# Hybrid diffusion backbone on one core: three in-projection tiles from inputs that are scaled but not yet shifted

## The chip, the cores and the metric

The kernel runs on one core of a Trainium2 chip. The core has a matrix engine (TensorE, PE in the profile), VectorE (DVE), ScalarE (ACT), GpSimd (POOL), and SyncE (SP), which here only issues transfers. Each engine takes its own instructions in the order in which the program lists them; between engines there are semaphores. The metric is the time of one execution on the device, in microseconds (us). Shares and rows come from one profiled execution.

## The reference

Two streams, 256 latent and 256 context tokens of width 1024, go through two layers. Each layer starts with an RMS norm whose result is scaled and shifted by vectors made from a conditioning vector (adaLN); layer 0 then has one large in-projection. What the change touches is this, for both streams:

```
mod_l = jnp.split((jax.nn.silu(c) @ ada_w[li] + ada_b[li])[:, None, :], 6, axis=-1)
mod_c = jnp.split(jax.nn.silu(c_ctx) @ ada_w[li] + ada_b[li], 6, axis=-1)
hl = rmsnorm(xl, norm1_g[li]) * (1.0 + mod_l[1]) + mod_l[0]
hc = rmsnorm(xc, norm1_g[li]) * (1.0 + mod_c[1]) + mod_c[0]
...
p_lat = h_lat @ w_in
p_ctx = h_ctx @ w_in
...
p = p + (centred_shift(p) - p) * mu
r, k, v, wd, ad, gd = jnp.split(p, ...)
```

`mod[0]` is the shift, `mod[1]` the scale; each is one vector of 1024 for a stream. `centred_shift` is the mean of the two neighbouring tokens. `wd` and `ad` then go through small matrices (lora) to a decay and a gate, `k` is normalised head by head (kk), and a recurrent scan follows, then attention heads, MLP, a second layer.

## The kernel before

Both streams lie side by side, 512 columns, 128 features on the partitions, so 1024 features are eight blocks j. Every product with weights is made in fp32 parts: a weight tile `rw` (four blocks k of 128x128, one DMA, L356) is copied to its high part `rh` on ACT (`actf`, L357, shown in the profile as L90) and the rest `rl` on DVE or POOL (L358); the input is split in the same way into `hh` and `hl`. `unit` multiplies one such half tile: for each of the four k, hh by rh, hl by rh, hh by rl, 12 matmuls of 128x512 into the PSUM tile `inps`. An in-projection tile is two halves (`in_half`), 24 matmuls. `w_ahead` prepares up to three half tiles ahead in the order of the list `todo`.

The start: the constants, x and ctx are loaded, then 16 pieces `araw` of 512 KB of the adaLN weights, for the shift (job (0,0)) and the scale (job (0,1)). `ada` (L180) multiplies them with `csil`, the conditioning after its silu: 32 fp32 matmuls for a job, each two records in the profile, into `adaps`. ACT copies the result to `adarow`, PE transposes it back with `ct` (a table of constants), DVE adds the bias and writes `mods`. From the scale DVE makes `gs` (gain times one plus scale). In the meantime the norms have made x times its reciprocal root, in place. Then for j in 8 and for both streams: `hh` = x·gs + shift on ACT, the same in full as `nap` on DVE (L413), `hl` = nap - hh on DVE (L414).

Then come the tables `cr` and `ca`, and a pool that takes over the space of x: the two small matrices `lora` and `gup` (L512, L514), the table `sm` (DVE, from `pk`), and a ring of four `arow` tiles (256 KB) through which three more adaLN jobs, (0,2) to (0,4), are loaded on SP's queue (L191) and multiplied bit by bit, one piece behind each step of `units`.

`units` is the list of in-projection tiles: `wda` (column 1536: wd and ad), then k, r, v of the four pairs of heads, then the gate. The PSUM tiles come from `bank`: two buffers called mm and one called x, in turn, so that a fourth tile takes the buffer of the first. `shiftmix` reads a finished tile: one ACT copy with the factor mu1, and two DVE operations over 510 columns that add the neighbours (the tiles are `wda` and `krv`). With wda, PE makes `zp` and `ap` (through lora), ACT `lt`, DVE two scans `cs`, POOL the products `BK`, `AR` and `bsum`. For kk, ACT squares k (`smq`), PE sums per head (`kkps`, eight records), DVE makes a reciprocal root in small Newton steps (`nw_x`, `nw_y`, `nw_t`), PE spreads it (`kkb`), DVE multiplies (`kk`). A table `after` says behind which step of `units` each of these is issued, so the program's order is written by hand, and every engine keeps it.

The first two tiles, wda and k of the first pair, are made together: half 0 of both, then half 1 of both.

Of the kernel before, what the change touches and what calls it, by code (L numbers as in the profile page):

```python
# [7 lines left out]
F32 = mybir.dt.float32  # L8
# [9 lines left out]
D = 1024  # L18
# [33 lines left out]
def build(ctx: ExitStack, tc, xT, cT, pk_d, ct_d, ca_d, cs_d, lora_d, gup_d, cb_d, ada_w, adaT, w_in, w_out, w1, w2,  # L52
# [24 lines left out]
    def tt(o, a, b, op):  # L77
        dve.tensor_tensor(o, a, b, op)  # L78

    def ts(o, a, s1, op0, s2=None, op1=None):  # L80
        if op1 is None:
            dve.tensor_scalar(o, a, s1, None, op0)
        else:
            dve.tensor_scalar(o, a, s1, s2, op0, op1)

    def stt(o, a, s, b, op0, op1):
        dve.scalar_tensor_tensor(o, a, s, b, op0, op1)  # L87

    def actf(o, i, f, scale=1.0, bias=0.0, **kw):
        act.activation(out=o, in_=i, func=f, scale=scale, bias=bias, **kw)  # L90

    def psm(shape, name="mm"):
        return PS["mm"].tile(shape, F32, name=name, tag="mm")
# [175 lines left out]
    def norm_add(acc, x):  # L269

        a, _, n = acc
        acc[2] += 1
        if n == 0:
            actf(a, x, AF.Square)
        else:
            sq = gen.tile([128, T], F32, name="sq", tag="sq" if n < 7 else "nap", bufs=2)
            actf(sq, x, AF.Square)
            if n < 7:
                tt(a, a, sq, ADD)
            else:  # L280
                acc[1] = sq
# [46 lines left out]
    with ExitStack() as c1:  # L328
# [12 lines left out]
            return reg.tile(shape, F32, name=name, tag="r4", bufs=6)  # L341

        wv = kview(w_in)
        todo, ready = [], []

        def w_unit():

# [3 lines left out]
        def w_ahead(n):  # L351
            while todo and len(ready) < n:
                v, c, k, eng = todo.pop(0)
                r, h, l = (reg.tile([128, 4, 128], dt, name=nm, tag=nm, bufs=b)
                           for nm, dt, b in (("rw", F32, 3), ("rh", F32R, 3), ("rl", F32R, 3)))
# [13 lines left out]
        def in_half(ps, i):  # L369
            unit(ps, hh, hl, 4 * i, i == 0, i == 1)  # L370

        def enqueue(v, cols, ks=(0, 4), engs=(pool,)):
            todo.extend((v, c, k, engs[i % len(engs)]) for i, c in enumerate(cols) for k in ks)

        for k in (0, 4):
            enqueue(wv, [1536, 512], (k,), (dve,))
        enqueue(wv, [0, 1024], (0, 4), (dve,))
# [6 lines left out]
        def split(src, hi, lo):  # L384
            actf(hi, src, AF.Copy)
            tt(lo, src, hi.bitcast(F32), SUB)

        with tc.tile_pool(name="x0", bufs=1) as xp:
            x0 = [xp.tile([128, 8, T], F32, name=f"x0{s}") for s in range(2)]
            nc.sync.dma_start(out=x0[0], in_=xT)  # L390
            nc.sync.dma_start(out=x0[1], in_=cT)
# [5 lines left out]
            gs = {}  # L397
            for s in range(2):
                acc = norm_acc(xp, s)
                for j in range(8):  # L400
                    norm_add(acc, x0[s][:, j])
                pb = norm_rstd(acc)
                for j in range(8):
                    tt(x0[s][:, j], x0[s][:, j], pb, MUL)
                gs[s] = gen.tile([128, 8], F32, name="gs", tag="gs", bufs=2)
                stt(gs[s], mods[0][:, 1, s], 1.0, PV("n1")[:, 0:8], ADD, MUL)
            for j in range(8):
                for s in range(2):
                    c = slice(s * T, s * T + T)
                    t = gen.tile([128, T], F32, name="nap", tag="nap", bufs=2)  # L410
                    m_ = gs[s][:, j:j + 1], mods[0][:, 0, s, j:j + 1]
                    actf(hh[:, j, c], x0[s][:, j], AF.Identity, scale=m_[0], bias=m_[1])
                    ts(t, x0[s][:, j], m_[0], MUL, m_[1], ADD)  # L413
# [93 lines left out]
        with tc.tile_pool(name="prep", bufs=1) as pp:  # L507
# [25 lines left out]
            rot = [0]  # L533

            def bank():

                rot[0] += 1
                return PS["x"].tile([128, NT], F32, name="inps", tag="x") if rot[0] % 3 == 0 else psm([128, NT], "inps")

            def shiftmix(n, o, ps=None):  # L540
                if ps is None:
                    ps = bank()
                    in_half(ps, 0)
                    yield
                    in_half(ps, 1)
                p3 = lambda a: a.rearrange("p (s t) -> p s t", s=2)
                actf(o, ps, AF.Identity, scale=mu1[:, n:n + 1])
                for i, j in ((slice(0, T - 1), slice(1, T)), (slice(1, T), slice(0, T - 1))):
                    stt(p3(o)[:, :, j], p3(ps)[:, :, i], muh[:, n:n + 1], p3(o)[:, :, j], MUL, ADD)

            def kk_norm(hp, k):

# [104 lines left out]

            def units():

                p2 = [bank() for _ in range(2)]  # L660
                for i in range(2):
                    for ps in p2:
                        in_half(ps, i)
                    yield
                yield from shiftmix(12, wda, p2.pop(0))
                actf(wda[0:64], wda[0:64], AF.Tanh)
                yield
                for hp in range(4):
                    krvs.append([])
                    for sec in (1, 0, 2):  # L670
                        krvs[hp].append(ring("krv", [128, NT], 6))
                        yield from shiftmix(4 * sec + hp, krvs[hp][-1], p2.pop() if p2 else None)
# [1015 lines left out]
```

## Time and profile before

| | us |
|---|---|
| runs | 1421.06, 1425.53, 1426.71 (median 1425.53) |
| the profiled execution, its own time | 1426.16 |
| its span | 1424.4 |
| PE busy | 1348.7 |
| DVE, ACT, POOL busy | 1046.4, 632.3, 264.5 |
| mean granted clock of TensorE | 0.974 |

The span is the time from the first instruction of the core to the last; starting and ending the program makes up the rest of the profiled execution's own time. Rows of groups give an operation as "out<-in", with partitions x elements and a type; a bracket behind a row of the timeline tells how long the engine had been idle and what released it. Helpers issue most instructions, so many rows have the same line (L75 matmul, L90 ACT, L78, L84 and L87 DVE); they are told apart by the tiles' names. In the timeline SPq is SP's queue of transfers and PEld the loading of weights.

### The profile page before, as it was taken

Reading aid. Unit: us, or ns where it says so; the run is one execution under the profiler, and the core shown is the slowest. Engines: PE = TensorE matmul, PEld = TensorE weight load, DVE = VectorE, ACT = ScalarE, POOL = GpSimd, SP = SyncE. Lnnn points to the kernel's source line nnn. Section 1 sums busy time; section 2 is a strip of 40 time slices with the busy share of each in tenths; the row PEclk is TensorE's granted clock in tenths of the full one; section 3 lists DMA queues with packets and bytes.
Section 4 is the critical chain, followed back from the end, with each engine's and each line's share of the span. In section 5 each row is a group of like instructions: output and inputs, shape, how many; then the busy total and the mean of one; then the engine's idle time right before and its main releaser. Section 6 shows DMA issues by size and latency. Waiting matters only on the chain.

```text
span 1424.4 us, 25962 instructions
## 1 busy us (share of the span) xinstructions
PE 1348.7 (95%) x10026; PEld 1139.4 (80%) x10026; DVE 1046.4 (73%) x2245; ACT 632.3 (44%) x1186; POOL 264.5 (19%) x196
## 2 busy tenths in 40 slices
PE   6899998999998799999999998999999989999997
PEld 2566666777887788888888997888888879999997
DVE  3788869756778899887666577697778785766665
ACT  2534434444543543223232243765645533555543
POOL 0122342211004200000000001233323335311100
PEclk9999998899999899999999999999999999999998
DMA  9566574134323466666666433754444423566663
GB/s 350 171 187 185 185 200 111 60 77 171 104 85 112 133 201 186 192 191 200 207 195 215 145 103 88 180 146 134 133 119 133 110 84 106 153 186 187 184 185 97
DMA packets 311324, 220.42 MB, mean 155 GB/s; under 512 B 30176, under 2 KB 279840, under 8 KB 310048
## 3 DMA queue, kind: packets, MB, share of 16 engines
q1 hardware_dynamic: 306080, 210.36, 49.8%
q10 hardware_dynamic: 3968, 4.20, 1.0%
q0 software_dynamic: 1152, 4.19, 0.8%
q8 instruction: 79, 1.29, 0.4%
q14 instruction: 45, 0.37, 0.1%
HBM read 205.54 MB, written 13.17 MB: 154 GB/s over the span
## 4 chain that ended last, share of the span: by engine, by line
PE 61%; DVE 5%; ACT 1%; issue 1%; DVEq 0%; ACTq 0%
PE m L75 38%; PE xsp L75 5%; PE zp L75 3%; PE bm L75 3%; PE so L75 3%; PE first L75 1%; PE cm L75 1%; PE ssdy L75 1%; PE hst L75 1%; PE xtp L1434 1%; PE nps L75 0%; DVE cva L87 0%; PE gn L75 0%; PE hlat L75 0%; PE gnb L75 0%
## 5 line engine op out<-in xcount | busy, mean ns | idle before, releaser
L90 ACT ACTIVATE wh<-wraw 128x1024 fp32r<-128x1024 f32 x197 | 208.2, 1058 | 366.4 <-PE m L75 255.6
L75 PE MATMUL m<-hid,wh 128*128 128x256 f32 (+1 forms) x1152 | 256.5, 318 | 0.6 <-DVE hid L78 0.6
L146 POOL TENSOR_TENSOR wl<-wraw,wh 128x1024 fp32r<-128x1024 f32 x55 | 133.2, 2428 | 614.5 <-ACT wh L90 602.5
L146 DVE TENSOR_TENSOR wl<-wraw,wh 128x1024 fp32r<-128x1024 f32 x142 | 173.7, 1223 | 43.8 <-ACT wh L90 43.7
L75 PEld LDWEIGHTS m<-hid,wh 128*128 128x128 f32 x1152 | 190.5, 189 | 17.0 <-DVE hid L78 0.8
L75 PE MATMUL m<-hid,wl 128*128 128x256 f32 (+1 forms) x576 | 183.3, 318 | 0.0
L75 PEld LDWEIGHTS m<-hid,wl 128*128 128x128 f32 x576 | 108.8, 189 | 7.7
L75 PE MATMUL m<-hh,wh 128*128 128x512 f32 (+1 forms) x264 | 103.3, 394 | 0.0
L75 PE MATMUL m<-hh,wl 128*128 128x512 f32 (+1 forms) x264 | 103.1, 393 | 0.0
L75 PE MATMUL m<-hl,wh 128*128 128x512 f32 (+1 forms) x264 | 103.1, 393 | 0.0
L246 DVE CUSTOM_DVE_ANT_0 arow<-arow,cb 128x512 f32<-128x512 f32 x112 | 75.9, 689 | 27.2 <-DMA arow<-in_adaT_dram 26.1
L358 POOL TENSOR_TENSOR rl<-rw,rh 128x512 fp32r<-128x512 f32 x45 | 59.9, 1333 | 187.2 <-ACT rh L90 177.2
L75 PE MATMUL inps<-hh,rh 128*128 128x512 f32 x208 | 90.2, 435 | 2.7 <-ACT hh L90 2.7
L90 ACT ACTIVATE rh<-rw 128x512 fp32r<-128x512 f32 x73 | 45.5, 627 | 95.2 <-PE inps L75 63.1
L75 PE MATMUL inps<-hl,rh 128*128 128x512 f32 x208 | 85.7, 413 | 0.2 <-DVE hl L78 0.2
L75 PE MATMUL inps<-hh,rl 128*128 128x512 f32 x208 | 85.2, 410 | 0.0
L75 PE MATMUL m<-uh,wh 128*128 128x258 f32 x256 | 73.4, 287 | 2.4 <-ACT uh L90 2.4
L75 PE MATMUL m<-ul,wh 128*128 128x258 f32 x256 | 73.3, 286 | 0.0
L75 PE MATMUL m<-uh,wl 128*128 128x258 f32 x256 | 73.2, 286 | 0.0
L75 PEld LDWEIGHTS m<-hh,wh 128*128 128x128 f32 x264 | 50.7, 192 | 11.2
L75 PEld LDWEIGHTS m<-hh,wl 128*128 128x128 f32 x264 | 50.5, 192 | 11.5
L75 PEld LDWEIGHTS m<-hl,wh 128*128 128x128 f32 x264 | 50.5, 192 | 11.1
(690 smaller groups left out, 3340.9 us busy)
## 6 DMA issues: line engine op xcount, KB each, us to landing
wraw<-in_w_dram SPq DMA_DIRECT2D x133, 512.0 KB, 3.9
arow<-in_adaT_dram SPq DMA_DIRECT2D x112, 256.0 KB, 3.3
wraw<-in_s_in_dram SPq DMA_DIRECT2D x48, 512.0 KB, 4.3
rw<-in_w_in_dram SPq DMA_DIRECT2D x52, 256.0 KB, 3.6
arow<-in_ada_w_dram SPq DMA_DIRECT2D x48, 256.0 KB, 3.5
araw<-in_ada_w_dram SPq DMA_DIRECT2D x16, 512.0 KB, 9.3
csb<-csd SPq DMA_DIRECT2D x8, 1024.0 KB, 6.3
wraw<-in_s_out_dram SPq DMA_DIRECT2D x16, 512.0 KB, 3.8
```

The source lines that it names most:

```text
L75: pe.matmul(o, lhsT=l, rhs=r, start=start, stop=stop)
L90: act.activation(out=o, in_=i, func=f, scale=scale, bias=bias, **kw)
L146: eng.tensor_tensor(l, raw, h.bitcast(F32), SUB)
L246: dve.tensor_tensor_reduce(r if s == ns - 1 else junk, r, cb[:, s, i * W:i * W + W], 0.5, 0.0, MUL, ADD, sums[:, s, j, i:i + 1])
L358: eng.tensor_tensor(l, r, h.bitcast(F32), SUB)
L1434: pe.transpose(tp[:, q, i * 128:i * 128 + 128], xs[:, i, t0:t0 + 128], ident)
```

## The change

The scale is computed first, the shift second. As soon as the scale is there, x·gs alone is split, without the shift: blocks 0 to 3 into `hh` and `hl`, blocks 4 to 7 into a tile `pv_` (ACT for the high part, one DVE operation for the rest). With these the first three tiles (columns 1536, 512 and 0, the list `p3`) are multiplied, half 0 from hh and hl, half 1 from pv_. The matmuls of the shift's job run among them. The weights of these three tiles stay as they were loaded, in six tiles `er` in the pool of the x0 section. When the shift is there, 24 small fp32 matmuls multiply it with er (`bps`, 128x2 each), ACT copies them to `bsb`, and `shiftmix` adds bsb to the three tiles per stream, 256 columns at a time, in PSUM. For all other tiles hh and hl are built again with the shift, as before. x0 moves to a space (`ar`) of a longer-lived pool and `pv_` to another (`bk`).

```
-            run((ada([(0, 0), (0, 1)], araw, D), 1))
+            A = ada([(0, 1), (0, 0)], araw, D)
+            run((islice(A, 5), 1))
             w_ahead(3)
+            run((islice(A, 4), 1))
...
             for j in range(8):
                 for s in range(2):
                     c = slice(s * T, s * T + T)
+                    g = gs[s][:, j:j + 1]
+                    ph, pl = (pv_[:, 0, j - 4, c], pv_[:, 1, j - 4, c]) if j > 3 else (hh[:, j, c], hl[:, j, c])
+                    actf(ph, x0[:, s, j], AF.Copy, scale=g)
+                    stt(pl, x0[:, s, j], g, ph.bitcast(F32), MUL, SUB)
+            p3 = [bank() for _ in range(3)]
+            for ps in p3:
+                unit(ps, hh, hl, 0, True, False)
+                run((islice(A, 3), 1))
+            run((A, 1))
+            w_ahead(3)
+            bps = psg([128, 3, 2], "bps")
+            for t in range(3):
+                for k in range(8):
+                    mm(bps[:, t], er[:, 3 * (k // 4) + t, k % 4], mods[0][:, 0, :, k], k == 0, k == 7)
+            actf(bsb, bps, AF.Copy)
+            for ps in p3:
+                unit(ps, pv_[:, 0], pv_[:, 1], 0, False, True)
+            for j in (0, 1, 2, 3, 4, 5, 6, 7):
...
-            def shiftmix(n, o, ps=None):
-                if ps is None:
+            def shiftmix(n, o):
+                if p3:
+                    i, ps = 3 - len(p3), p3.pop(0)
+                    for s in range(2):
+                        c = slice(s * T, s * T + T)
+                        actf(ps[:, c], ps[:, c], AF.Identity, bias=bsb[:, i, s:s + 1])
+                else:
                     ps = bank()
...
             def units():
 
-                p2 = [bank() for _ in range(2)]
-                for i in range(2):
-                    for ps in p2:
-                        in_half(ps, i)
-                    yield
-                yield from shiftmix(12, wda, p2.pop(0))
+                yield
+                yield
+                yield from shiftmix(12, wda)
```

On PE, behind the transposition that ends the first adaLN job, there stood before:

```order
L75 MATMUL adaps<-ct,adarow 128x8 x2
L75 MATMUL adaps<-araw,csil 32x256 x32
L75 MATMUL adaps<-ct,adarow 128x8 x2
L75 MATMUL inps<-hh,rh 128x512 x2
L75 MATMUL inps<-hl,rh 128x512
```

and now:

```order
L75 MATMUL adaps<-ct,adarow 128x8 x2
L75 MATMUL inps<-hh,rh 128x512 x3
L75 MATMUL adaps<-araw,csil 32x256
L75 MATMUL inps<-hl,rh 128x512
L75 MATMUL inps<-hh,rl 128x512
```

The first products now come right behind the first transposition, and the 32 matmuls (64 records) of the second job are spread among them.

Further on PE, where the shift is ready, and then where the three tiles end and the fourth begins, the changed order has (the names ending in a number are tiles of that name: pv_ and mods):

```order
L75 MATMUL adaps<-ct,adarow 128x8 x2
L75 MATMUL inps<-pv__98,rh 128x512
L75 MATMUL inps<-pv__98,rl 128x512
L75 MATMUL bps<-mods_79,er 128x2 x24
L75 MATMUL inps<-pv__98,rh 128x512 x2
...
L75 MATMUL inps<-pv__98,rl 128x512
L75 MATMUL adaps<-arow,csil 32x2x64 x44
L75 MATMUL inps<-hh,rh 128x512
```

The 24 matmuls of bps stand ahead of the last 27 products of the three tiles, and 44 matmuls on arow, which were spread among products before in pieces of four and eight, stand in one row ahead of the fourth tile.

On ACT, at the same place of the program, before:

```order
L90 ACTIVATE adarow<-adaps 128x256 x2
L90 ACTIVATE rh<-rw 128x512
L90 ACTIVATE hh<-x_100,mods_79,gs 128x256
L90 ACTIVATE rh<-rw 128x512 x2
L90 ACTIVATE hh<-x_101,mods_79,gs 128x256
```

and now, from the second adarow on:

```order
L90 ACTIVATE adarow<-adaps 128x256
L90 ACTIVATE rh<-er 128x512 x2
L90 ACTIVATE hh<-x_97,mods_79,gs 128x256
L90 ACTIVATE bsb<-bps 128x6
L90 ACTIVATE hh<-x_97,mods_79,gs 128x256
L90 ACTIVATE rh<-rw 128x512
L90 ACTIVATE hh<-x_97,mods_79,gs 128x256 x4
L90 ACTIVATE rh<-rw 128x512
L90 ACTIVATE hh<-x_97,mods_79,gs 128x256 x10
L90 ACTIVATE inps<-inps,bsb 128x256 x6
L90 ACTIVATE wda<-inps,sm 128x512
```

The copy of bps stands between the first and the second hh with the shift; the other fifteen come behind it, and the six additions of bsb behind them.

On DVE, in the changed program, from kkps's result to the last Newton step:

```order
L84 TENSOR_SCALAR nw_x<-kkps 128x8
L84 TENSOR_SCALAR nw_y<-nw_x 128x8
L84 TENSOR_SCALAR lt<-lt 128x512
L78 TENSOR_TENSOR nw_t<-nw_y,nw_x 128x8
L641 SCALAR_TENSOR_TENSOR cs<-cr,lt 128x256 x2
L78 TENSOR_TENSOR nw_t<-nw_t,nw_y 128x8
...
L78 TENSOR_TENSOR nw_t<-nw_t,nw_y 128x8
L87 SCALAR_TENSOR_TENSOR bsum<-bsum,sm,krv 128x256
L87 SCALAR_TENSOR_TENSOR nw_y<-nw_t,nw_y 128x8
```

The scans cs and the operations on lt, which all stood ahead of nw_x before, now stand among the Newton steps.

More of the change, by code (lines that the diff above doesn't have):

```diff
@@ L353, in w_ahead @@
                 v, c, k, eng = todo.pop(0)
-                r, h, l = (reg.tile([128, 4, 128], dt, name=nm, tag=nm, bufs=b)
-                           for nm, dt, b in (("rw", F32, 3), ("rh", F32R, 3), ("rl", F32R, 3)))
+                r, h, l = (raws_.pop(0) if raws_ and nm == "rw" else reg.tile([128, 4, 128], dt, name=nm, tag=nm, bufs=3)
+                           for nm, dt in (("rw", F32), ("rh", F32R), ("rl", F32R)))
                 nc.sync.dma_start(out=r, in_=v[:, k:k + 4, c:c + 128])
@@ L375, in build @@
         for k in (0, 4):
[L376 to L377 removed]
+            enqueue(wv, [1536, 512, 0], (k,), (dve,))
+        enqueue(wv, [1024], (0, 4), (dve,))
         for hp in range(1, 4):
@@ L386, in split, with bank @@
             tt(lo, src, hi.bitcast(F32), SUB)
+        rot = [0]
+        def bank():
+            rot[0] += 1
+            return PS["x"].tile([128, NT], F32, name="inps", tag="x") if rot[0] % 3 == 0 else psm([128, NT], "inps")
+        x0 = mid.tile([128, 2, 8, T], F32, name="x0", tag="ar")
+        pv_ = mid.tile([128, 2, 4, NT], F32R, name="pv_", tag="bk")
+        bsb = reg.tile([128, 3, 2], F32, name="bsb")
         with tc.tile_pool(name="x0", bufs=1) as xp:
-            x0 = [xp.tile([128, 8, T], F32, name=f"x0{s}") for s in range(2)]
-            nc.sync.dma_start(out=x0[0], in_=xT)
-            nc.sync.dma_start(out=x0[1], in_=cT)
+            for s, v in enumerate((xT, cT)):
+                nc.sync.dma_start(out=x0[:, s], in_=v)
+            er = xp.tile([128, 6, 4, 128], F32, name="er")
+            raws_.extend(er[:, i] for i in range(6))
             i = iter(range(16))
             araw = lambda sh, n: r4(sh, n) if next(i) % 3 else xp.tile(sh, F32, name=n, tag="araw", bufs=3)
-            run((ada([(0, 0), (0, 1)], araw, D), 1))
+            A = ada([(0, 1), (0, 0)], araw, D)
+            run((islice(A, 5), 1))
             w_ahead(3)
+            run((islice(A, 4), 1))
             hh, hl = halloc()
-            gs = {}
+            gs = []
             for s in range(2):
@@ L400, in build @@
                 for j in range(8):
-                    norm_add(acc, x0[s][:, j])
+                    norm_add(acc, x0[:, s, j])
                 pb = norm_rstd(acc)
                 for j in range(8):
-                    tt(x0[s][:, j], x0[s][:, j], pb, MUL)
-                gs[s] = gen.tile([128, 8], F32, name="gs", tag="gs", bufs=2)
+                    tt(x0[:, s, j], x0[:, s, j], pb, MUL)
+                gs.append(gen.tile([128, 8], F32, name="gs", tag="gs", bufs=2))
                 stt(gs[s], mods[0][:, 1, s], 1.0, PV("n1")[:, 0:8], ADD, MUL)
@@ L409, in build @@
                     c = slice(s * T, s * T + T)
+                    g = gs[s][:, j:j + 1]
[18 more added lines that the diff above has]
+                    c = slice(s * T, s * T + T)
                     t = gen.tile([128, T], F32, name="nap", tag="nap", bufs=2)
                     m_ = gs[s][:, j:j + 1], mods[0][:, 0, s, j:j + 1]
-                    actf(hh[:, j, c], x0[s][:, j], AF.Identity, scale=m_[0], bias=m_[1])
-                    ts(t, x0[s][:, j], m_[0], MUL, m_[1], ADD)
+                    actf(hh[:, j, c], x0[:, s, j], AF.Identity, scale=m_[0], bias=m_[1])
+                    ts(t, x0[:, s, j], m_[0], MUL, m_[1], ADD)
                     tt(hl[:, j, c], t, hh[:, j, c].bitcast(F32), SUB)
@@ L532, in build @@
                 pool.memset(e[:, :, 65:66], 1.0)
[L533 to L538, printed above, removed]
-            def shiftmix(n, o, ps=None):
-                if ps is None:
+            def shiftmix(n, o):
+                if p3:
+                    i, ps = 3 - len(p3), p3.pop(0)
+                    for s in range(2):
+                        c = slice(s * T, s * T + T)
+                        actf(ps[:, c], ps[:, c], AF.Identity, bias=bsb[:, i, s:s + 1])
+                else:
                     ps = bank()
@@ L671, in units @@
                         krvs[hp].append(ring("krv", [128, NT], 6))
-                        yield from shiftmix(4 * sec + hp, krvs[hp][-1], p2.pop() if p2 else None)
+                        if hp == 0 and sec == 0:
+                            yield
+                        yield from shiftmix(4 * sec + hp, krvs[hp][-1])
                         yield
```

6 lines of the change are left out of this document (3 added, 3 removed).

## The prediction

> **What bounds the kernel now.** I read the page first (busy shares, the 40 slices), then the time in windows around the in-projection, then TensorE's waits there, then the timeline row by row.
>
> ```profile
> PE 1348.7 (95%) x10026; PEld 1139.4 (80%) x10026; DVE 1046.4 (73%) x2245; ACT 632.3 (44%) x1186; POOL 264.5 (19%) x196
> ...
> PE   6899998999998799999999998999999989999997
> ```
>
> TensorE (PE) is busy 95% of the span, and only the first slices leave it much room. The change works between 28 and 92 us, so I cut that stretch into stages (columns: window, its length, busy time of PE, weight loads, DVE, ACT, POOL, granted clock, DMA share, GB/s).
>
> ```profile
> 27.90:35.30 7.40, 7.40 (x64) 2.09 (x63) 0.18 (x1) 0.00 (x0) 0.00 (x0) 1.00 0.95 310
> 35.30:39.30 4.00, 0.72 (x9) 0.55 (x5) 2.59 (x8) 3.11 (x7) 0.00 (x0) 1.00 0.07 23
> 39.30:43.10 3.80, 3.63 (x9) 2.48 (x10) 3.80 (x12) 3.80 (x9) 0.00 (x0) 0.56 0.69 193
> 43.10:54.20 11.10, 11.08 (x47) 8.36 (x45) 10.30 (x34) 6.22 (x13) 0.22 (x4) 1.00 0.36 123
> 54.20:92.50 38.30, 37.49 (x326) 24.44 (x325) 27.41 (x49) 16.59 (x37) 10.04 (x10) 1.00 0.72 218
> 92.50:200.00 107.50, 105.24 (x856) 74.47 (x856) 78.11 (x147) 44.56 (x100) 36.33 (x38) 1.00 0.59 179
> ```
>
> PE works 98% of every window except the second, and in the third it gets 0.56 of its clock. What ended PE's waits between 27.8 and 92.6:
>
> ```profile
> PE inps L75 <- ACT hh L90: 2.7, 1, 2.7
> PE adaps L75 <- ACT adarow L90: 0.6, 1, 0.6
> PE adaps L75 <- DMA arow<-in_ada_w_dram: 0.6, 1, 0.6
> PE zp L75 <- ACT TT L90: 0.2, 1, 0.2
> PE inps L75 <- DVE hl L78: 0.2, 1, 0.2
> ```
>
> That is 4.3 us of waits. In the third window the clock costs 3.8 x 0.44 = 1.7 us more. **So 6.0 us is all that a better order can win here**; anything that it adds to PE is to be set against this.
>
> **The start.** Rows of the timeline (start, duration, engine, line, operation, tiles, count, idle time before and its releaser):
>
> ```profile
> 27.79 7.59 PE L75 MATMUL adaps<-araw,csil 128*32 128x256 f32 x64
> 27.97 0.18 DVE L78 TENSOR_TENSOR mods<-adaps,pk 128x16 f32<-128x16 f32 x1 [1.32 <-PE adaps L75]
> ...
> 36.67 0.17 DVE L78 TENSOR_TENSOR mods<-adaps,pk 128x16 f32<-128x16 f32 x1 [8.53 <-PE adaps L75]
> ...
> 38.63 7.48 ACT L90 ACTIVATE hh<-x,mods,gs 128x256 fp32r<-128x256 f32 x15
> 39.27 0.87 PE L75 MATMUL inps<-hh,rh 128*128 128x512 f32 x2 [2.70 <-ACT hh L90]
> ```
>
> From the second vector (36.67) to the first product (39.27) it is 2.6 us. In the changed order the scale comes first, so its vector is there at 27.97, and the first product stands at 30.6, with the same 2.7 us gap on PE: the 64 matmuls for the shift, which filled 27.79 to 35.38, now stand in PE's order *behind* the first products, and PE takes its instructions in order. The early gap is therefore moved, not closed. What goes is the second transposition's 0.6, the 0.2 for hl and, because of other waits below, the 0.6 for arow and 0.2 for zp: **-1.6 us**.
>
> The clock went with the gap:
>
> ```profile
> 40.00:41.00 1.00, 0.83 (x3) 0.60 (x3) 1.00 (x4) 1.00 (x3) 0.00 (x0) 0.50 0.49 129
> ```
>
> After the 2.70 us gap PE ran at 0.50. Elsewhere in the same trace a gap as long left the clock alone:
>
> ```profile
> 430.71 0.36 PE L75 MATMUL wo<-mh,rh 128*128 128x256 f32 x1 [2.73 <-DVE x L87]
> 430.70:433.43 2.73, 2.72 (x17) 2.44 (x18) 2.49 (x8) 1.10 (x3) 0.39 (x1) 1.00 0.59 182
> ```
>
> So a gap of this length may or may not be followed by half the clock. The gap at 28 is as that at 37: PE idles but for one transposition. I leave the 1.7 us where they were: 0. If the clock stays up, 1.7 us are won; if it falls behind a later gap too, 1.7 are lost. The Trainium skill (TensorE: Matmul & The Clock Gate, "Part 1: The HAM clock gate") has the half clock set in after at least one idle window of about 3.4 us, on windows that run free; taken literally, 2.7 us would never be enough, and this trace disagrees once (0.50 behind 2.70 us) and agrees once (1.00 behind 2.73 us). By that rule the sum below would be 1.7 us less.
>
> **What is added on DVE and ACT before the shift is there.** Sixteen more copies on ACT (15 took 7.48, 0.50 each: 8.0 us) and sixteen products x·gs - hh on DVE.
>
> ```profile
> L84 DVE TENSOR_SCALAR nap<-x,gs,mods x16: 405/408/411, 37.6 to 48.4; 128x256 f32<-128x256 f32 x16
> L78 DVE TENSOR_TENSOR hl<-nap,hh x16: 417/418/422, 39.5 to 49.1; 128x256 fp32r<-128x256 f32 x16
> ```
>
> The nearest rows are these 0.41 and 0.42 us, so 6.7 us. Both engines stand idle in 27.90:35.30 (0.18 and 0.00 busy of 7.40), and that hides them: 0. Without this cover, 6.7 us at most. The six er tiles are 1.5 MB loaded in front of or between the last araw tiles; 1 MB of it at 310 GB/s is 3.4 us that the last araw comes later, but PE reaches that one near 50 instead of 35: 0.
>
> **The 24 small matmuls (bps).** The bias needs er times shift in full fp32, two records each, 48 records with 2 columns. The trace has the same kind in kkps:
>
> ```profile
> 64.73 0.95 PE L75 MATMUL kkps<-cr,smq 128*128 128x2 f32 x8
> 65.60 1.12 PE L75 MATMUL adaps<-arow,csil 128*32 128x128 f32 x16
> 66.65 0.50 PE L75 MATMUL inps<-hh,rh 128*128 128x512 f32 x1
> 66.99 0.40 PE L75 MATMUL inps<-hl,rh 128*128 128x512 f32 x1
> 67.22 0.40 PE L75 MATMUL inps<-hh,rl 128*128 128x512 f32 x1
> ```
>
> Eight records take 0.87 until the next row starts, 0.109 each. 48 x 0.109 = **+5.2 us** on PE, with no other work beside it. The bounds are the nearest rows: 0.066 a record as in arow (1.05 for 16), 3.2; 0.119 by the row's whole 0.95, 5.7. I take kkps, whose shape it is. A product inps takes 0.23 (66.99 to 67.22), and 0.11 more behind small matmuls (66.65 to 66.99); with as much on the way in, an estimate, a visit of small matmuls costs 0.2 beside its records.
>
> Where this stands: 30.6 + 64 shift matmuls (7.4) + 45 of the 72 products of the three tiles (10.5) + the transposition (0.5) + six visits at 0.2 (1.2) + the cold clock 1.7 = 51.9. bps ends at B = **57.1**.
>
> **First new wait: the fourth tile.** ACT's copy bsb<-bps stands between the first and the second shifted hh. Fifteen hh, all hl behind them on DVE, six half-tile bias adds and the three shiftmixes queue behind the end of bps, B. The fourth tile takes the bank of the first one (two banks plus one take turns), so it waits for the last wda operation on DVE.
>
> ```profile
> 51.78 1.53 DVE L87 SCALAR_TENSOR_TENSOR wda<-inps,sm,wda 128x510 f32<-128x510 f32 x2
> ...
> 60.48 0.84 ACT L90 ACTIVATE lt<-zp,sm 128x256 f32<-128x256 f32 x2 [4.05 <-PE zp L75]
> ```
>
> On DVE: from the first nap (37.6) to the last hl (49.1 + 0.4) there are 11.9 us for 16 pairs with two weight parts rl among them, 0.74 a pair; 15.5 pairs make 11.5. Small sm operations 0.6, then wda, krv, wda at 0.76: 2.3. That is B + 14.4. ACT delivers at the same time: 0.2 + 15 x 0.50 + two rh at 0.6 + six adds at 0.42 + wda and krv 1.2 = 12.6, and the two rh wait about a microsecond for buffers that the products behind bps give back. So B + 14.4 to 15.5.
>
> In the meantime PE has 27 products (6.3) and, standing ahead of the fourth tile, 44 small matmuls on eleven arow tiles (88 records at 0.066, 5.8): 12.1 us. The gap is 2.3 to 3.4.
>
> **Second new wait, at the same place: arow.** SP's loads of lora, gup and arow lie in space that er leaves, and wait for bps too.
>
> ```profile
> 48.90 0.34 SPq L512 DMA_DIRECT2D lora<-in_lora_dram  x1
> ...
> 54.81 0.65 PE L75 MATMUL adaps<-arow,csil 128*32 128x128 f32 x8 [0.56 <-DMA arow<-in_ada_w_dram]
> ...
> DMA to landing us min/median/max: 2.6/3.6/5.6
> ```
>
> From lora's issue to the first arow matmul 5.9 us. Now lora goes out at B, not 48.90. Ring of four: tiles 1 to 4 at B + 5.9, 5 to 8 one reload later (3.6 + 0.5), 9 to 11 another, and three tiles' matmuls: 5.9 + 4.1 + 4.1 + 1.6 = B + 15.7. At 2.6 a reload it is 13.7, at 5.6 it is 19.7. Both chains thus end by B + 15.5, either one covers the other, and I take **+3.4 us** (1.6 to 7.6). Seven separate visits of arow become one, six saved where six came in above: 0.
>
> **Third new wait: kkb.** In the old trace kkps ended at 65.6 and kkb, behind Newton steps on DVE, began 7.0 us later.
>
> ```profile
> 65.09 1.28 POOL L633 TENSOR_TENSOR BK<-lt,cs 128x512 f32<-128x512 f32 x1 [15.86 <-DVE lt L78]
> 66.34 1.19 POOL L642 TENSOR_TENSOR bsum<-lt 128x256 f32<-128x256 f32 x1
> 68.52 1.52 POOL L635 TENSOR_TENSOR AR<-krv,e 128x256 f32<-128x256 f32 x2 [0.99 <-DVE nw_t L78]
> ...
> 68.47 1.01 DVE L87 SCALAR_TENSOR_TENSOR bsum<-bsum,sm,krv 128x256 f32<-128x256 f32 x1
> ...
> 72.64 1.09 PE L75 MATMUL kkb<-ct,nw_y 128*64 128x128 f32 x16
> ```
>
> Then PE had 31 products, and 32 small records, to fill these 7.0 us. Now between kkps and kkb stand 19 products and a zp: 4.8 us. On DVE the steps are strewn among lt, the two scans cs, rl and bsum, and bsum waits for POOL, where AR (1.52) and BK (1.28) now stand ahead of it (1.19): I count 8.8 instead of 7.0. The gap is 2.2 to 4.0; **+3.5 us**.
>
> **The sum.** -1.6 + 5.2 + 3.4 + 3.5 = **+10.5 us**. Behind kkb the rows of both orders soon agree, and with PE at 98% (92.50:200.00) a delay has nowhere to be made good. By the clock: kkb ends at B 57.1 + 15.5 + 3.7 (five products, zp, ap and kkps) + 8.8 + 1.1 = 86.2. In the old trace 18.8 us lay between kkb's end and
>
> ```profile
> 92.50 0.61 PE L75 MATMUL adaps<-ct,adarow 128*128 128x8 f32 x4
> ```
>
> of which some 2.2 us, nine products with what lies between them, have now gone in front of it; 86.2 + 16.6 = 102.8, a delay of 10.3. Of the two I take **+10.4 us**. The profiled execution took 1426.16 us (span 1424.4), 0.6 over the median of 1425.53. 1425.53 + 10.4 gives **1436 us**.
>
> **Rivals.**
> 1. *The filler is enough (not slower).* PE never starves behind bps, since its early products ran while DVE and ACT stood idle, and since hh and hl, which ACT and DVE rebuild, need not be complete for a tile to begin. Price: -1.6 + 5.2 = +3.6, 1429.1; with the gap at 28 us and its cold clock closed as well (2.7 + 1.7), -0.8, 1424.7. For it: PE's share is 98% everywhere else. Against: the copy bsb stands ahead of 15 hh, and both chains at B + 15.5 against 12.1 us of work. It decides where the two later gaps together stay under 3.5 us (7.1 - 3.6). Chance 0.24.
> 2. *arow lands late.* At 5.6 a reload the eleven tiles end at B + 19.7 instead of 15.5: +10.4 + 4.2 = +14.6, 1440.1, and 1441.8 with half the clock behind the gap. For it: 5.6 is in the row. Against: the median is 3.6. Chance 0.15.
> 3. *The clock stays up behind the first gap*, as at 430.71: +10.4 - 1.7 = +8.7, 1434.2. Chance 0.10.
> 4. *The change wins*, the three tiles being out of the way before the shift arrives: for over 0.5% it would have to save 7.1 us; 6.0 are there, and bps takes 5.2. Chance 0.03.
>
> That the change doesn't do what it says is excluded by the order of PE's rows: the products stand ahead of the shift.
>
> **How the numbers follow.** The forecast, +8 to +12, has 0.48. Range: rival 1's upper part at the low end (1427.5), rival 2 at the high end (1441.5). 0.5%, 7.1 us, is about what a measurement can tell from no change. Slower by more: nearly all of the forecast (0.43), rival 2 (0.15) and most of rival 3 (0.08): 0.66. Within: rival 1 and the lower edges, 0.30. Faster: 0.04.
>
> **What would show it.** Right: first inps near 30.6 with a 2.7 us wait; a bps row of 5 to 6 us ending near 57; lora issued just then; PE waiting for arow, then for kkb; the transposition of 92.50 near 102. Wrong: PE's wait list from 55 to 90 adds up to under 4 us, bps under 3 us, or lora issued before bps ends.

## The result and the profile after

| | before | changed |
|---|---|---|
| median of the runs, us | 1426.03 (4 runs, 1421.06 to 1426.71) | 1446.03 (4 runs, 1443.96 to 1449.19) |
| ratio, 95% interval | | 1.0136 [1.0111, 1.0160] |
| span of the profiled execution, us | 1424.4 | 1443.9 |
| PE busy, us | 1348.7 | 1361.4 |

The changed kernel is slower by 20 us. That is the direction of the forecast, but twice its size (+10.4), and outside its range. The page of the changed kernel, busy time and share by engine:

```profile
PE 1361.4 (94%) x10074; PEld 1147.9 (80%) x10074; DVE 1051.6 (73%) x2261; ACT 641.4 (44%) x1209; POOL 264.7 (18%) x196
```

What TensorE waited for there between 26 and 125 us (total, times, longest):

```profile
PE adaps L75 <- DMA arow<-in_ada_w_dram: 3.4, 3, 1.4
PE kkb L75 <- DVE nw_y L87: 2.7, 1, 2.7
PE inps L75 <- ACT hh L90: 2.5, 1, 2.5
PE zp L75 <- ACT wda L90: 1.2, 1, 1.2
```

The waits are about those that were forecast: 2.5 at the first product, 3.4 for arow, 2.7 for kkb. With two more, of 0.5 and 0.2, they are 10.5 us together, where the kernel before had 4.8 in the same stretch (24.4 to 101.9 us there), and so cannot be the surprise. TensorE's busy time has grown by 12.7 us although only 48 records were added. The timeline of TensorE in the changed kernel shows where:

```profile
28.86 0.61 PE L75 MATMUL adaps<-ct,adarow 128*128 128x8 f32 x4 [0.50 <-ACT adarow L90]
31.99 1.65 PE L75 MATMUL inps<-hh,rh 128*128 128x512 f32 x3 [2.52 <-ACT hh L90]
...
55.07 7.96 PE L75 MATMUL bps<-mods,er 128*128 128x2 f32 x48
62.88 1.20 PE L75 MATMUL inps<-pv__98,rh 128*128 128x512 f32 x2
...
71.62 2.05 PE L75 MATMUL adaps<-arow,csil 128*32 128x128 f32 x32
75.04 1.28 PE L75 MATMUL adaps<-arow,csil 128*32 128x128 f32 x16 [1.36 <-DMA arow<-in_ada_w_dram]
...
81.70 0.50 PE L75 MATMUL inps<-hh,rh 128*128 128x512 f32 x1
...
94.28 1.13 PE L75 MATMUL kkb<-ct,nw_y 128*64 128x128 f32 x16 [2.72 <-DVE nw_y L87]
...
115.59 0.61 PE L75 MATMUL adaps<-ct,adarow 128*128 128x8 f32 x4
```

bps takes 7.81 us (62.88 - 55.07), 0.163 a record and not 0.109. The 27 products behind it take 8.74 (71.62 - 62.88), not 6.3. The row of 92.50 stands at 115.59, +23.1 (+21.5 when both are measured from the first transposition, at 27.25 and 28.86). The granted clock in windows of the same profile (window, length, busy time of PE, weight loads, DVE, ACT, POOL, granted clock, DMA share, GB/s):

```profile
30.80:36.80 6.00, 4.81 (x10) 2.84 (x11) 5.98 (x15) 6.00 (x16) 0.00 (x0) 0.50 0.96 308
55.10:57.60 2.50, 2.50 (x25) 2.50 (x24) 2.06 (x5) 0.49 (x1) 0.00 (x0) 1.00 0.02 7
57.70:67.40 9.70, 9.70 (x37) 8.73 (x37) 2.57 (x7) 3.26 (x7) 0.22 (x4) 0.50 0.35 109
67.60:71.60 4.00, 4.00 (x17) 2.93 (x16) 2.23 (x6) 2.89 (x6) 0.00 (x0) 0.96 0.49 182
95.40:101.80 6.40, 6.40 (x24) 4.40 (x24) 5.77 (x12) 2.94 (x6) 0.00 (x0) 0.50 0.28 83
```

TensorE is 100% busy from 55 on, and yet 2.6 us into bps its clock falls to half, and stays there for 10 us. The half clock comes also at the first gap, where it now lasts 6.8 us (30.4 to 37.2) instead of 3.4, and behind the wait for kkb.

These changes come in steps. Cut into windows of 3.413 us with one edge at 57.66, the stretch from 20 to 1420 us has 410 of them, and in each the clock is 1.00 or 0.50 and never between; the same holds for the kernel before, with an edge at 39.72. So the 2.6 us are not a threshold: they are the place in bps at which a step came. In the other six profiles of kernels whose bps has two columns the fall comes 1.6 to 4.1 us behind the start of bps.

So two theories went into the experiments. **N**: matmuls with two columns stream so little that the clock treats TensorE as idle; bps lowers the clock on itself and on what follows. **W**: each bps record is slow since it loads a new fp32 weight block, and the clock falls for another reason. The experiments on the waits ask in addition what makes the fourth tile late: arow, or the hold, which is the time for which ScalarE keeps the building of hh and hl waiting. In the trace of each run I read when a row comes; times of runs are medians, against 1425.3 to 1426.8 of the kernel before on the same chip.

### The profile page after: what moved, and what is told of

Read it like the earlier page. It is cut to its first block, busy times and chain, and to the rows that moved or that the text cites. A ratio compares the mean times of both kernels' runs of the same rounds, so it can differ in the third digit from the quotient of the medians.

```text
span 1443.9 us, 26083 instructions
## 1 busy us (share of the span) xinstructions
PE 1361.4 (94%) x10074; PEld 1147.9 (80%) x10074; DVE 1051.6 (73%) x2261; ACT 641.4 (44%) x1209; POOL 264.7 (18%) x196
## 4 chain that ended last, share of the span: by engine, by line
PE 59%; DVE 5%; ACT 1%; issue 1%; DMA 0%; POOL 0%; DVEq 0%; ACTq 0%; POOLq 0%
PE m L75 37%; PE xsp L75 5%; PE zp L75 3%; PE bm L75 3%; PE so L75 1%; PE first L75 1%; PE cm L75 1%; PE ssdy L75 1%; PE hst L75 1%; PE xtp L1466 1%; DVE cva L87 0%; DVE ul L87 0%; PE nps L75 0%; DVE acc L78 0%; PE gn L75 0%
## 5 line engine op out<-in xcount | busy, mean ns | idle before, releaser
L75 PE MATMUL inps<-hh,rh 128*128 128x512 f32 x196 | 85.5, 438 | 2.5 <-ACT hh L90 2.5
L90 ACT ACTIVATE rh<-rw 128x512 fp32r<-128x512 f32 x67 | 42.0, 628 | 93.4 <-PE inps L75 56.6
L75 PE MATMUL inps<-hl,rh 128*128 128x512 f32 x196 | 81.0, 413 | 0.0
L75 PE MATMUL inps<-hh,rl 128*128 128x512 f32 x196 | 80.2, 409 | 0.0
L75 PEld LDWEIGHTS m<-hh,wh 128*128 128x128 f32 x264 | 50.9, 193 | 11.2
## 6 DMA issues: line engine op xcount, KB each, us to landing
araw<-in_ada_w_dram SPq DMA_DIRECT2D x16, 512.0 KB, 10.2
```

Of the source, the lines that this page charges most:

```text
L75: pe.matmul(o, lhsT=l, rhs=r, start=start, stop=stop)
```

## Experiments

**1. Without bps.** The matmuls and the copy are replaced by zeros.

```
-            bps = psg([128, 3, 2], "bps")
...
-            actf(bsb, bps, AF.Copy)
+            pool.memset(bsb, 0.0)
```

> Leaves out the shift's part in the three early tiles: no bps matmuls, bsb is zero. Read at the transposition row that stood at 92.50 before and at 115.59 in the changed kernel. Theory N (narrow matmuls let TensorE's clock fall): what goes is the 7.8 us of bps and the 2.4 us that the products behind it lost at half clock; these products then end near 61.5 instead of 71.6, the arow loads go out near 56 instead of 63, and the row stands near 107 (-8 to -10); granted clock 1.00 from 55 to 63. Rival W (bps is slow because each record reloads fp32 weights, and the half clock has another cause): -5 to -6, and the products behind still run at half clock.

Measured: 1437.6 us, ratio to the kernel before 1.0090 [1.0060, 1.0120]. Lora is issued at 56.05. The window over the 27 products in this run:

```profile
54.50:61.40 6.90, 6.83 (x29) 5.17 (x28) 6.82 (x19) 6.64 (x14) 0.32 (x4) 1.00 0.55 175
```

The clock holds. In its timeline the transposition of 115.59 stands at

```profile
104.81 0.61 PE L75 MATMUL adaps<-ct,adarow 128*128 128x8 f32 x4
```

10.8 us earlier, with the first transposition where it was (28.80). N gave 8 to 10, W 5 to 6. With what it holds up behind it, bps thus costs twice the 5.2 us at which I had priced it; and 12.3 us of the 23.1 are not its own. This is read from the rows: the times are 8.5 us apart, but the two intervals overlap at their edges (1.0111 and 1.0120).

**2. bps with 64 times the columns.** The same weights, each shift column repeated 64 times.

```
-            bps = psg([128, 3, 2], "bps")
+            bps = psg([128, 3, 2, 64], "bps")
...
-                    mm(bps[:, t], er[:, 3 * (k // 4) + t, k % 4], mods[0][:, 0, :, k], k == 0, k == 7)
+                    mm(bps[:, t], er[:, 3 * (k // 4) + t, k % 4],
+                       mods[0][:, 0, :, k:k + 1].to_broadcast([128, 2, 64]), k == 0, k == 7)
```

> The same 24 matmuls on the same weights, but with the two shift columns each repeated 64 times, so 128 columns instead of 2; nothing else is left out. Theory N: 64 times the columns and yet faster: the 48 records take 5 to 6.3 us instead of 7.8 and the granted clock stays at 1.00 through them and the products behind them (6.3 instead of 8.7 us). Rival W: at least the same 7.8 us, clock 0.50 behind as before.

Measured: 1437.4 us, 1.0072 [1.0048, 1.0096]: clear of the changed kernel's 1.0136 [1.0111, 1.0160]. The row of bps in this run's timeline, and its windows over bps and over the products behind it:

```profile
52.15 5.56 PE L75 MATMUL bps<-mods,er 128*128 128x128 f32 x48
```

```profile
52.20:57.50 5.30, 5.30 (x50) 5.30 (x49) 5.30 (x16) 5.30 (x11) 0.00 (x0) 1.00 0.01 3
57.70:64.20 6.50, 6.50 (x36) 4.89 (x34) 6.50 (x19) 5.61 (x13) 0.22 (x4) 1.00 0.83 266
```

More work on the same weights, and it is faster: 5.56 instead of 7.96 us, at clock 1.00 to the end. The weight loads are the same 48, so W falls and N stands. All the profiles agree: in the seven whose bps has two columns the clock falls within bps, in the three with 128 columns (experiments 2, 9 and 11) it stays at 1.00 to its end. Nor is it the rest of the other engines: in experiment 8 ScalarE and VectorE work all through bps, and with two columns the clock falls all the same. The order behind bps changed too in this kernel (20 arow matmuls in a row, not 44, and hh ahead of bsb), so only the rows of bps and of the clock are laid to the columns alone, and not the whole 8.6 us.

**3. Only 32 columns.** As before, with 16 in place of 64, which leaves the order nearly alone.

> As the run with 128 columns, but each shift column only 16 times: 32 columns instead of 2, with nearly the changed kernel's own order (40 arow matmuls in a row instead of 44). Theory N, if it is the number of columns that keeps the clock up by degrees: between the two, 48 records in 5.5 us and the clock at 1.00 if 32 columns are enough, 7 to 8 us with 0.50 from about 3 us on if they are not. If the clock stays up, kkb starts 4 to 5 us earlier than the changed kernel's 94.28, with the order left as it is. Rival W: 7.8 us either way.

The row of bps and two windows over it:

```profile
53.99 7.30 PE L75 MATMUL bps<-mods,er 128*128 128x32 f32 x48
```

```profile
54.00:56.60 2.60, 2.60 (x25) 2.60 (x25) 2.60 (x7) 1.49 (x3) 0.00 (x0) 1.00 0.03 6
57.50:61.30 3.80, 3.80 (x19) 3.80 (x20) 0.00 (x0) 0.00 (x0) 0.00 (x0) 0.50 0.00 0
```

Measured: 1442.4 us, 1.0111 [1.0085, 1.0137]. 32 columns are not enough: full clock at first, then half, as with two. A record of 128 columns costs 0.066 us in the arow rows and one of narrow columns, like kkps, 0.109 at full clock. So 128 columns fill at most some 60% (0.066 / 0.109) of TensorE's time in bps and 32 columns some 15%, both estimates. Where between them the clock turns was not tried.

**4. The copy bsb behind the hh.** One instruction moves on ScalarE; the line `actf(bsb, bps, AF.Copy)` stands behind the loop that builds hh and hl.

> Only the copy bsb<-bps moves on ScalarE from between the first and second shifted hh to behind the sixteenth. hh and hl are then built from 55 to 67 instead of from 63 to 78. If the hold of hh sets the start of the fourth tile (81.70 in the changed kernel), that start comes 4 us or more earlier. If the arow matmuls ahead of it set it (their last piece lands at 79.7), it stays within 1 us of 81.7 and the row of 115.59 within 1 us.

Measured: 1450.0 us, 1.0163 [1.0129, 1.0197], the fourth tile at 82.95, 53.9 after the first transposition (52.8 in the changed kernel), and the row at 115.47. Nothing is won. ScalarE's rows in the changed kernel, and those of a later run with the copy moved (experiment 7), tell why:

```profile
63.06 0.18 ACT L90 ACTIVATE bsb<-bps 128x6 f32<-128x6 f32 x1 [7.47 <-PE bps L75]
63.13 0.59 ACT L90 ACTIVATE hh<-x,mods,gs 128x256 fp32r<-128x256 f32 x1
64.17 0.63 ACT L90 ACTIVATE rh<-rw 128x512 fp32r<-128x512 f32 x1 [0.45 <-ACT hh L90]
...
68.71 0.63 ACT L90 ACTIVATE rh<-rw 128x512 fp32r<-128x512 f32 x1 [1.94 <-PE inps L75]
```

```profile
63.28 0.63 ACT L90 ACTIVATE rh<-rw 128x512 fp32r<-128x512 f32 x1 [7.99 <-issue]
```

Right behind the second hh stands a copy of the next weights, rh<-rw. It needs one of three rh buffers, and these come free only when products behind bps have read them: the profile names such a product as releaser of the later copy, at 68.71, and none for the one at 63.28. With bsb out of the way ScalarE stands in front of this copy just as long, 7.99 us for 7.47.

**5. er in a space of its own.**

```
+        erp = cp.enter_context(tc.tile_pool(name="erp", bufs=1))
...
-            er = xp.tile([128, 6, 4, 128], F32, name="er")
+            er = erp.tile([128, 6, 4, 128], F32, name="er")
```

> The er tiles get a space of their own, so lora and arow need not wait for bps: lora is issued near 55 instead of 63.05, TensorE no longer waits for arow (3.4 us in the changed kernel). If arow sets the fourth tile, it starts 4 us or more earlier than 81.70. If the hold of hh by bsb sets it (the last wda operation ends at 80.2), it starts near 80.3, 1.4 us earlier, and the row of 115.59 comes to 114.

Measured: 1443.0 us, 1.0118 [1.0094, 1.0141], not to be told from the changed kernel. The queue of transfers in this run and in the changed kernel:

```profile
52.49 0.33 SPq L548 DMA_DIRECT2D lora<-in_lora_dram  x1
...
53.34 23.87 SPq L191 DMA_DIRECT2D arow<-in_ada_w_dram  x11
```

```profile
63.05 0.33 SPq L547 DMA_DIRECT2D lora<-in_lora_dram  x1
...
63.91 14.48 SPq L191 DMA_DIRECT2D arow<-in_ada_w_dram  x11
```

The loads begin 10.6 us earlier, and yet their row ends at the same place, 49.5 us behind the first transposition (27.71 here) in both, and TensorE still waits 3.4 us for arow. The fifth arow needs a buffer of the ring of four, and gets it when TensorE has used the first, which it does only behind all products of the three tiles: four loads are issued at once, the fifth at 71.3 (72.3 in the changed kernel), each time 0.7 us behind TensorE's first arow matmul. It is the ring that makes arow late, not the late start.

**6. and 7. No arow ahead of the fourth tile; alone (arow_later), and with the copy bsb late (hold_and_arow).**

```
-                    if u > 1:
+                    if u > 6:
                         next(A, None)
```

> The changed kernel, with the arow matmuls begun five steps later, so that none stands ahead of the fourth tile (their 5.8 us come later). If the hold of hh by bsb is a second cause as late as arow, the fourth tile starts near 80.3 (wda's last operation), 1.4 us earlier than 81.70, TensorE idles 8 us there, and the time is 2 to 5 us longer. If arow alone made it late, the fourth tile starts near 72 and the time is 3 us shorter.

> Both at once: the copy bsb behind the sixteenth hh, and no arow ahead of the fourth tile. If each covered the other, the fourth tile starts at 72 to 75 and kkb 6 to 9 us earlier than 94.28, and the time is 2 to 4 us shorter than the changed kernel's 1446 (5.8 us of arow work come later). If neither matters, the fourth tile stays near 80.

Measured: 1454.3 us, 1.0206 [1.0181, 1.0230], and 1456.7 us, 1.0208 [1.0179, 1.0236]. TensorE's timeline, first without arow alone and then with both edits:

```profile
80.27 0.77 PE L75 MATMUL inps<-hh,rh 128*128 128x512 f32 x1 [8.68 <-DVE wda L87]
```

```profile
79.59 0.77 PE L75 MATMUL inps<-hh,rh 128*128 128x512 f32 x1 [8.68 <-DVE wda L87]
```

The hold is a second cause as late as arow (80.27, as expected of it), and bsb alone is not what makes it: with bsb late the same 8.68 us. The times are longer than I had thought, 8 and 11 us more than the changed kernel's, instead of 2 to 5 more and of a gain. Part of it is the clock again: with nothing to do in this wait TensorE has 0.50 from 74.0 to 87.7 in both runs, where the changed kernel has 1.00. It works 7.4 us of that in arow_later, half of which, 3.7 us, is an estimate of the loss.

**8. All hh ahead of the weight copies (hh_first_arow).** As 7, but the loop that builds hh and hl stands in front of the products behind bps, so that ScalarE's copies rh<-rw come behind it.

> As hold_and_arow (no arow ahead of the fourth tile, copy bsb late), but all sixteen shifted hh also stand ahead of ScalarE's next weight copies rh<-rw, which wait for one of three rh buffers that the products behind bps give back. If these copies are the hold, hh and hl are done by 67, under bps, and the fourth tile starts at 73 to 75 instead of 79.6, and the time is 4 to 6 us shorter than the 1454 to 1457 of the two runs without arow. If the hold lies elsewhere, the fourth tile stays near 79.6.

The timeline of ScalarE and of TensorE in this run:

```profile
54.84 7.97 ACT L90 ACTIVATE hh<-x,mods,gs 128x256 fp32r<-128x256 f32 x16
```

```profile
75.81 0.77 PE L75 MATMUL inps<-hh,rh 128*128 128x512 f32 x1 [4.21 <-DVE wda L87]
```

Measured: 1451.6 us, 1.0181 [1.0157, 1.0205]. All sixteen hh run under bps, and the fourth tile starts 46.3 us after the first transposition, not 50.9. So the copies were a hold behind bsb, and half of the 8.68 us: with bsb alone out of the way nothing goes, with both 4.5 us. The copies alone, with bsb left in its place, were not tried. The 4.21 us that stay are in ScalarE's queue too: its wda copy, at 72.88, stands behind a bias addition that waits for the third tile's products until 71.63. The time is 5 us below that of 7, with intervals that overlap.

**9. 128 columns, bsb late, arow three steps later (combo4).**

> 128 columns for bps, the copy bsb last, arow begun three steps later. By theory N with both waits gone: bps 5.6 us at full clock, fourth tile by 66 to 68, time 1432 to 1436, still above the 1426.8 of the kernel before, since bps stays and the first gap of 2.5 us too. If the waits are made up elsewhere: 1437, as with 128 columns alone.

Measured: 1443.7 us, 1.0128 [1.0106, 1.0150], so slower than with the columns alone. The fourth tile waits 4.31 us for wda until 70.72, with no arow matmuls to fill the wait, and the clock is at 0.50 for 10.2 us from 69.8 on: as in 6, moving arow away costs more than it gives.

**10. Four matmuls into the first gap (warm).** The changed kernel with matmuls that nobody reads.

```
+            fo = psg([128, 2, 256], "fill")
+            for _ in range(4):
+                mm(fo, ident, mods[0][:, 1, :, 0:1].to_broadcast([128, 2, 256]))
             p3 = [bank() for _ in range(3)]
```

> The changed kernel with four more matmuls of 128x512 in the 2.5 us gap ahead of the first product, into a bank that nobody reads (about 0.5 us each, from arow's 0.066 a record of 128 columns). Theory N (the clock follows how much TensorE has streamed): the granted clock stays at 1.00 from 30 to 37 instead of 0.50, and bps starts 2 to 3.4 us earlier after the first transposition than the 26.2 us of the changed kernel. Rival (a gap's length alone decides, or the stall of the products does): the clock falls all the same and nothing is won.

TensorE's timeline in this run, and a window over the products behind the gap:

```profile
30.24 3.70 PE L75 MATMUL fill<-mods,ct 128*128 128x512 f32 x8 [0.34 <-DVE mods L78]
...
52.09 6.57 PE L75 MATMUL bps<-mods,er 128*128 128x2 f32 x48
```

```profile
33.40:37.00 3.60, 3.60 (x18) 2.36 (x20) 3.60 (x10) 3.60 (x10) 0.00 (x0) 1.00 1.15 287
```

The clock stays up, as N has it and its rival has not, and bps begins 22.8 us after the first transposition (29.29) instead of 26.2: 3.4 us won by added work, the upper end of what N gave. Not all of it is the clock. The order changed too: the shift's matmuls come in three groups among the products here and in six in the changed kernel. And the place of the steps counts: in the ten profiles of the changed kernel and its variants without the filler the half clock at this gap lasts 3.4 us in five and 6.8 in the other five. In the changed kernel 5.2 us of work ran at half clock there, which is 2.6 us, an estimate. Measured: 1440.2 us, 1.0111 [1.0086, 1.0137], an interval that overlaps the changed kernel's; the gain is read from the rows, not from the times.

**11. All three (c_hh_warm):** the edits of 2, 8 (with arow left where the change has it) and 10.

> 128 columns for bps, hh ahead of the weight copies, and the four matmuls in the first gap. If all three causes are named rightly they add up: no half clock up to 100, fourth tile at 63 to 66, time 1431 to 1434 against 1437.4 with the columns alone; still above the kernel before by bps (5.6 us) less what the early products save.

Measured: 1435.2 us, 1.0053 [1.0034, 1.0071]. There is no half clock up to 69, where one of 3.4 us follows a wait of 1.5 us for arow (expected was none up to 100). The fourth tile starts at 67.16, the row of 115.59 stands at 101.77. It is the best of the changed kernels, more than half of the loss is gone, and it is still slower than the kernel before.

**12. The kernel before with such matmuls (before_fill).** At the first gap, at the norm's sums near 481, and at the three group norms of layer 1.

```
+    def fill(n, rhs=None):
+        o = psg([128, 512], "fill")
+        for _ in range(n):
+            mm(o, ident, pk[:, 0:512] if rhs is None else rhs)
...
+        if nf:
+            fill(nf)
...
             r = rsqrt(np_, 1.0 / 256, EPS, n, "gr")
+            fill(4)
```

> The kernel before, without the change, with matmuls of 128x512 into a bank that nobody reads: four ahead of the first product, five ahead of the norm's sums at 481 (gap 3.8 us), four at each of the three group norms of layer 1. Theory N: each clock drop of 1.7 to 5.1 us that follows these places (40, 480 to 490, 1040, 1152, 1186) goes, less what the added matmuls take where the gap is shorter than they: 4 to 10 us faster than before, 1417 to 1422. If gaps are not what lowers the clock: 0 to 6 us slower.

Measured: 1428.3 us, 1.0017 [1.0002, 1.0032]: no gain, where N let me expect 4 to 10 us. A window over the group norm's stretch of layer 1 in the kernel before, and then in this run:

```profile
1040.00:1046.00 6.00, 6.00 (x20) 5.03 (x19) 1.84 (x11) 2.37 (x4) 0.36 (x1) 0.50 0.83 262
```

```profile
1040.00:1046.00 6.00, 6.00 (x59) 5.71 (x59) 4.43 (x7) 6.00 (x16) 2.39 (x1) 1.00 0.30 76
```

and the added matmuls at the norm near 481 in this run's timeline:

```profile
485.43 2.90 PE L75 MATMUL fill<-pk,ct 128*128 128x512 f32 x3 [3.79 <-DVE nap L87]
```

The mean granted clock rose from 0.974 to 0.983, which over 1424 us is worth 12.8 us, an estimate; but the 42 added records take 0.39 us each (8 of them 3.14, from 37.04 to 40.18), 16.5 us, of which the gaps hide a part. At 481 they waited with the norm, as the row's bracket shows, and came behind the gap. A filler that costs what the low clock costs is no gain, and no version here beats the kernel before.

## Why the prediction was right or wrong

*The start.* The first product was put at 30.6 with the gap of 2.7 us kept; it came at 31.99 with 2.52, because the first transposition came at 28.86 instead of 27.25. Over all profiles of the changed family (the changed kernel and the variants above) it stands between 26.83 and 29.56, so I can't lay these 1.6 us to the er loads; that stays open. The gap was moved, not closed, as forecast.

*The clock*, **the step that failed**. "I leave the 1.7 us where they were: 0" held neither for the first gap nor for anything behind it. The half clock at the first gap lasted twice as long: up to bps it took 1.6 us more, of which 0.9 is the clock (half of 5.2 us of work, where 1.7 us was reckoned) and the rest is not told apart. bps itself was priced from the kkps rows at "0.109 each"; those are eight records in a full-clock stretch, behind which the clock stayed at 1.00, while 48 lowered it on themselves (7.8 for 5.2 us, +2.6) and on the 27 products (8.7 for 6.3, +2.4). Behind the wait for kkb it fell again (20.2 us from kkb's end to the transposition, where 16.6 was reckoned, +3.6). With 1.6 at the start and 1.0 between bps and the fourth tile and elsewhere these are the 12.8 us between the forecast 102.8 and the measured 115.59. Some 9 of the 12.8 are clock. Experiments 1 and 2 show the two terms of bps. Experiment 10 shows that work in the first gap keeps the clock up, but not the size of that term alone; for kkb the clock's row alone speaks. The two terms of bps came in every profile with two columns. Of the other two a part is luck: both times the half clock lasted 6.8 us in this profile, while others of the changed family have 3.4 in the same places. Rival 3 had the clock rise where it sank; no rival had a busy TensorE lower it.

The kernel before had shown both already. Three of its windows, cut at the steps of its own clock (39.72 is one), and a row of the third:

```profile
36.31:39.72 3.41, 0.71 (x5) 0.46 (x4) 3.01 (x9) 2.74 (x7) 0.00 (x0) 1.00 0.18 53
428.84:432.25 3.41, 1.54 (x12) 1.48 (x12) 3.38 (x7) 0.00 (x0) 1.26 (x1) 1.00 0.52 146
1036.41:1039.82 3.41, 3.41 (x26) 3.19 (x26) 1.30 (x3) 3.41 (x10) 1.83 (x1) 1.00 0.70 187
```

```profile
1037.17 0.95 PE L75 MATMUL gn<-ct,gsq 128*128 128x1 f32 x8
```

The first holds the whole gap of 2.70 us, which leaves 0.71 us of work, and the next window is at 0.50. The gap of 2.73 us, on which the prediction left the question open, falls across two windows, the second of which, shown here, still has 1.54 us of work: the clock stays at 1.00. By this it is the gap's place that decides, not its length alone. In the third window TensorE is busy all the time, but 20 of the 26 records are of one column, and from 1039.82 on the clock is at 0.50 (the stretch shown in experiment 12). A busy TensorE with a lowered clock thus stood in the trace from which the prediction was made; it was sought only behind gaps. How much narrow work it takes is not settled: the 1.8 us of these rows in the third window were enough, 1.6 us of the same rows in a window of the changed kernel (1061.18 to 1064.59) were not.

The Trainium skill (TensorE: Matmul & The Clock Gate, "What's actually happening") ties the half clock to how busy TensorE has been in a window of 3413 ns. The lengths here agree: the low stretches last some 3.4, 6.8 and 10 us. The table there gives an idle window as the cause, and I had read it as a window without matmuls; here a window with 0.71 us of work, or a full one of narrow matmuls, was enough.

*First new wait.* Its size (fourth tile at B + 14.4 to 15.5) nearly held: arow_later has it at 80.27, 16.8 us behind the end of a bps that was followed by half clock. Its named cause was only the first of several: behind bsb stand the weight copies, which hold ScalarE as long (experiments 4 and 7), and behind them the bias additions (experiment 8). I had seen these copies wait "about a microsecond" and put the rest on bsb.

*Second new wait.* +3.4 forecast, 3.4 measured. That the sizes agree is luck, for the path was another: lora does lie in er's space (63.05, at the end of bps, as forecast), but freeing it won nothing. The ring of four and eleven tiles in a row are the cause. "Either one covers the other" held, for the ring's wait and the hold: without arow (6) the fourth tile came 2.1 us earlier after the first transposition, with bsb late (4) 1.0 us later.

*Third new wait.* +3.5 forecast, 2.7 measured, and 1.2 for wda, whose ScalarE row stood behind a weight copy that waited for its load. The "31 products" that PE is said to have had between kkps and kkb are a miscount: the old trace has 19 there, as the new one has. The number entered no term of the sum.

*Behind the row.* The forecast carried the delay to the end: "a delay has nowhere to be made good". At TensorE's first and last product with hid, before and changed:

```profile
L75 PE MATMUL m<-hid,wh x1152: 276/283/398, 577.2 to 1412.9; 128*128 128x256 f32 x128, 128*128 128x512 f32 x64
```

```profile
L75 PE MATMUL m<-hid,wh x1152: 277/283/398, 601.7 to 1432.6; 128*128 128x256 f32 x128, 128*128 128x512 f32 x64
```

24.5 us late at 577 and 19.7 at the end: 4.8 us were made good in layer 1, in rows that did not change. It is the clock once more: between these two products the profile before has 34.2 us at 0.50, the changed one 23.9, and ten us at half clock are some five of work. In the stretch that shows 0.50 before (1040 to 1046, above), the changed kernel has

```profile
1064.50:1070.50 6.00, 5.92 (x34) 4.59 (x33) 2.85 (x14) 2.34 (x4) 0.33 (x1) 1.00 0.84 267
```

So a shift of the whole program changes how its gaps and narrow matmuls fall into the windows of the clock; where a single profile ends is open to some microseconds by that alone.

*The rivals.* "The filler is enough" needed the later gaps under 3.5 us: they were 7.3 with wda's. It would not have been reached without the clock either: c_hh_warm, with full clock to 69, loses 0.5%. "arow lands late" did not come, its wait was the 3.4 us of the forecast. That the change could win was priced at 6.0 us against 5.2 for bps, and this bound held: nothing here came below the kernel before.

## What to carry to other kernels

Price a run of matmuls by its columns and its length: here 48 records with few columns lowered the clock each time, eight did not, and what followed paid as well. Find the steps at which the granted clock changes, cut the trace at them, and ask of each window how much of it is work on many columns, whatever the busy share says; the same work on more columns can be faster. And where an engine is held, test each waiting row in its queue: behind the first stood a second that waited for the same thing.

## What was not expected of the hardware

Besides the clock under a busy TensorE (half with 2 and with 32 columns, full with 128) and its steps of 3.413 us: small operations on VectorE took several times as long while GpSimd worked. In the changed kernel's timeline, GpSimd's AR and BK, and VectorE's Newton steps on 128x8 beside them and behind them:

```profile
89.19 2.23 POOL L668 TENSOR_TENSOR AR<-krv,e 128x256 f32<-128x256 f32 x2 [25.88 <-ACT e L90]
91.38 1.26 POOL L666 TENSOR_TENSOR BK<-lt,cs 128x512 f32<-128x512 f32 x1
```

```profile
90.80 0.65 DVE L78 TENSOR_TENSOR nw_t<-nw_y,nw_x 128x8 f32<-128x8 f32 x1
91.48 1.19 DVE L78 TENSOR_TENSOR nw_t<-nw_t,nw_y 128x8 f32<-128x8 f32 x1
92.70 0.65 DVE L87 SCALAR_TENSOR_TENSOR nw_y<-nw_t,nw_y 128x8 f32<-128x8 f32 x1
93.38 0.17 DVE L78 TENSOR_TENSOR nw_t<-nw_y,nw_x 128x8 f32<-128x8 f32 x1
```

0.65, 1.19 and 0.65 us where each takes 0.17 else: about 2 us of the wait for kkb. It is the same from 60 to 126 us in all fourteen profiles: a Newton step with no work of GpSimd beside it takes 0.17 us at most, and all those of 0.6 us and more have such work beside them, though a few stay at 0.17 even so. That GpSimd is the reason is still argued from the coincidence; no run took its work away.
